# A channel mixer in two token halves, with gate and up products in Strassen's form, on one Trainium2 core

## Chip, cores and metric

One core of a Trainium2 chip runs the whole program. Its engines run side by side: TensorE (PE: matmuls; PEld: its weight loads), VectorE (DVE), ScalarE (ACT), GpSimd (POOL), and SyncE (SP), which here issues the DMAs. The metric is the time of one execution on the device in microseconds (us); lower is better. TensorE's granted clock has two levels, 1.2 and 2.4 GHz; the profile gives it as a share of the upper one.

## What is computed

Two layers over 1152 tokens (128 prompt and 1024 sample tokens) of 1024 features. Each layer is a token mixer (latent attention, short convolution, retention, not changed in what it computes) and a SwiGLU channel mixer with 2816 hidden features, both with a modulated norm and a gated residual:

```
def _swiglu(h, w_gate, w_up, w_down):
    return (jax.nn.silu(h @ w_gate) * (h @ w_up)) @ w_down
...
xs = xs + g1 * mix
xs = xs + g2 * _swiglu(_modulate(_rmsnorm(xs, norm2_g[l]), sh2, sc2), *ffn)
```

Everything is float32; prompt tokens have another modulation (shift, scale, gate) than sample tokens.

## The kernel before

Activations lie feature-major: a tile is 128 features by 1152 tokens, and the residual x is 8 such tiles. Each large product runs as three matmuls on operands that were split into a rounded part and a rest, hi and lo (type float32r): `mm3` (L189 to L194) issues hi*hi, hi*lo and lo*hi for each 128 features of the contraction and adds them up in a PSUM tile. A matmul's moving operand is a chunk of 384 tokens; there are three chunks, taken in the order 1, 2, 0 at a phase's boundaries.

Weights come in tiles of 128 x 1024 from a queue written out by hand (`order`, L93). `prep_next` (L142) loads the next one on SP, copies it to hi on ACT (L169) and subtracts on POOL to get lo (L170); `get` keeps one more key prepared than the one in use. The tiles rotate through a pool of 7 (`W`); activations rotate through a pool of 34 slots of 128 x 1152 (`S`), small pieces through 8 temporaries (`Tt`). PSUM's eight banks are two pools, `mm` (3) and `ax` (5).

The channel mixer has 22 hidden tiles in groups of 2 or 3. `gate_up` (L1291) makes one hidden tile: three gate products of 24 matmuls each, with silu on ACT (L1280), then three up products, multiplied in on DVE (L1285), and split on ACT (L1286) and DVE (L1287). After a group has been made, `down` (L1306) adds the group before it to the residual: for each of 8 output tiles and 3 chunks one PSUM tile of 6 or 9 matmuls, and one or two DVE operations (`resid`, L1200; two for chunk 0, where prompt and sample tokens have different gates). The order in which the engines get their instructions is that of a scheduler which follows the program's order but lets a later instruction go first where, by its own estimate, an earlier one still waits.

`boundary` (L1237) carries the three chunks through the end of one phase (`rows_tail`, the last products that are added to the residual), the norm (squares on ACT, sums on DVE and POOL L391, 1/sqrt in small DVE steps L201 to L206, spread over the partitions by PE L247), its application (L422 to L429), and the first products of the next phase. It is used twice in a layer: from the output projection to the channel mixer, and from the channel mixer to the next layer. In layer 0's mixer the modulations of layer 1 are computed on the side (`tick`, `ada_work`).

Of the kernel before, what the change touches and what calls it, by code (L numbers as in the profile page):

```python
# [29 lines left out]
GROUPS = [2, 3, 3, 3, 3, 3, 3, 2]  # L30
EPS = 1e-6
SCALE = 96.0 ** -0.5
NS, NW = 34, 7          # slots of [128, 1152] and of [128, 1024]
# [10 lines left out]
M0, M1, M2 = 3, 5, 6  # L44


def segs(c):
    if c == 0:
        return [(0, 128, 0), (128, 384, 1)]
    return [(c * CH, (c + 1) * CH, 1)]  # L50


class Net:
    def __init__(self, ctx, tc, a, o):
# [5 lines left out]
        self.tp = pool("temps", bufs=8)  # L60
# [32 lines left out]
    def order(self):  # L93
        q = []
        for l in range(L):
            q += [("in", l, i) for i in range(len(IN_FM))]
            q += [("woa", l, m) for m in range(8)] + [("wob", l, j) for j in range(2)]
            h = 0
            for gi, g in enumerate(GROUPS):
                for i in range(g):  # L100
                    if h != 1:
                        q += [("gate", l, h), ("up", l, h)]
# [16 lines left out]
    def wsrc(self, key):  # L119
# [8 lines left out]
        if k == "gate":  # L128
            return a["w_gate"][l, key[2]], 1024
# [1413 lines left out]
```

## Time and profile before

| | us |
|---|---|
| median of three runs | 3245.52 |
| lowest, highest run | 3243.17, 3247.36 |
| the profiled execution, first to last instruction (span) | 3242.0 |
| TensorE busy in the span | 3136.6 (97%) |
| VectorE busy | 1407.3 (43%) |
| ScalarE busy | 956.3 (29%) |
| GpSimd busy | 860.1 (27%) |

The page gives the profiled execution by its span; the timed runs lie 1.2 to 5.4 us above it. A busy share is that of one engine over the whole span. A matmul's row shows a start and a modelled duration; matmuls overlap in the pipeline, so the step from one start to the next is what a matmul costs. The same holds, in a smaller measure, for DVE.

### The profile page before, as it was taken

What the parts mean: (1) busy time and instruction counts of PE and PEld (TensorE: products, weight loads), DVE (VectorE), ACT (ScalarE), POOL (GpSimd) and SP (SyncE); (2) the same over time, 40 slices, a digit from 0 to 9 for tenths busy, and PEclk for the clock granted to TensorE, in tenths of its full rate; (3) what the DMA queues carried; (4) which work ended last, traced back from release to release, by engine and by line L of the source; (5) the groups of instructions that cost most, each with busy time, mean ns of one, the idle gap of its engine ahead of it and who ended that gap; (6) DMA issues with size and microseconds to landing.
All of it is one profiled execution on the core that took longest, in us unless ns stands there. A gap on an engine that the chain in (4) does not pass through costs nothing.

```text
span 3242.0 us, 43302 instructions
## 1 busy us (share of the span) xinstructions
PE 3136.6 (97%) x17680; PEld 2785.3 (86%) x17680; DVE 1407.3 (43%) x2914; ACT 956.3 (29%) x2388; POOL 860.1 (27%) x469
## 2 busy tenths in 40 slices
PE   6999989999999999999999999899999999999999
PEld 5988755578999999999989896555889999999999
DVE  6254576745422212312373646767364222223323
ACT  4433455433311111111144234454342111111110
POOL 3101344553212111211141113435441112111211
PEclk8999999999999999999999999999999999999999
DMA  5223100121121222222131110001211111111112
GB/s 212 99 72 127 34 12 16 36 101 45 46 77 61 71 82 69 65 80 76 60 119 34 33 53 12 12 30 59 76 34 33 35 49 41 40 43 49 40 40 85
DMA packets 75302, 191.18 MB, mean 59 GB/s; under 512 B 7264, under 2 KB 33632, under 8 KB 75104
## 3 DMA queue, kind: packets, MB, share of 16 engines
q1 hardware_dynamic: 75104, 188.42, 17.5%
q8 instruction: 139, 2.28, 0.3%
q14 instruction: 59, 0.48, 0.0%
HBM read 171.45 MB, written 16.94 MB: 58 GB/s over the span
## 4 chain that ended last, share of the span: by engine, by line
PE 87%; DVE 9%; ACT 2%; issue 1%; DMA 1%; SPq 0%; POOL 0%; ACTq 0%; POOLq 0%; DVEq 0%
PE mm L192 22%; PE mm L194 22%; PE mm L193 22%; PE ax L1071 5%; PE ax L1042 2%; PE mm L1088 2%; PE mm L1090 2%; PE mm L1089 2%; PE ax L303 1%; PE ax L1031 1%; DVE mx L1044 1%; PE ax L247 1%; DMA aw<-in_ada_w 1%; PE ax L921 1%; DVE rst L205 1%
## 5 line engine op out<-in xcount | busy, mean ns | idle before, releaser
L192 PE MATMUL mm<-hh,W 128*128 128x384 f32 x2720 | 919.8, 338 | 0.0
L194 PE MATMUL mm<-hh,W 128*128 128x384 f32 x2720 | 914.9, 336 | 0.0
L193 PE MATMUL mm<-hl,W 128*128 128x384 f32 x2720 | 914.6, 336 | 0.2
L170 POOL TENSOR_TENSOR W<-W,W 128x1024 fp32r<-128x1024 f32 (+1 forms) x190 | 420.5, 2213 | 1687.8 <-ACT W L169 1523.8
L192 PEld LDWEIGHTS mm<-hh,W 128*128 128x128 f32 x2720 | 513.1, 189 | 24.0 <-issue 17.3
L193 PEld LDWEIGHTS mm<-hl,W 128*128 128x128 f32 x2720 | 513.4, 189 | 2.2 <-POOL hl L429 0.8
L194 PEld LDWEIGHTS mm<-hh,W 128*128 128x128 f32 x2720 | 513.3, 189 | 1.3 <-issue 1.0
L1200 DVE SCALAR_TENSOR_TENSOR x<-mm,mod,x 128x384 f32<-128x384 f32 (+2 forms) x640 | 314.9, 514 | 367.5 <-PE mm L194 367.2
L169 ACT CAST W<-W 128x1024 fp32r<-128x1024 f32 (+1 forms) x190 | 185.8, 978 | 874.8 <-PE mm L193 797.8
L1285 DVE TENSOR_TENSOR sil<-sil,mm 128x384 f32<-128x384 f32 x132 | 73.0, 553 | 822.3 <-PE mm L194 820.5
L192 PE MATMUL mm<-gh,W 128*128 128x384 f32 x1056 | 353.9, 335 | 3.9 <-DVE x L1200 3.9
L194 PE MATMUL mm<-gh,W 128*128 128x384 f32 x1056 | 352.9, 334 | 1.2 <-POOL W L170 1.2
L193 PE MATMUL mm<-gl,W 128*128 128x384 f32 x1056 | 352.9, 334 | 0.0
L1080 POOL TENSOR_TENSOR pacc<-pacc,W 128x1024 f32<-128x1024 f32 x96 | 230.6, 2402 | 216.1 <-ACT W L1091 205.2
L1044 DVE TENSOR_REDUCE mx<-ax 128x1 f32<-128x384 f32 x384 | 195.0, 549 | 107.8 <-PE ax L1042 105.7
L1091 ACT ACTIVATE W<-mm 128x512 f32<-128x512 f32 x288 | 169.5, 607 | 211.8 <-PE mm L1090 198.8
L1071 PE MATMUL ax<-W,vt 128*64 128x512 f32 x576 | 204.6, 649 | 8.2 <-DVE attn L1123 6.7
L192 PEld LDWEIGHTS mm<-gh,W 128*128 128x128 f32 x1056 | 198.2, 188 | 8.7 <-issue 3.3
L194 PEld LDWEIGHTS mm<-gh,W 128*128 128x128 f32 x1056 | 198.2, 188 | 1.5 <-POOL W L170 1.5
L193 PEld LDWEIGHTS mm<-gl,W 128*128 128x128 f32 x1056 | 198.3, 188 | 0.0
L1286 ACT CAST gh<-sil 128x384 fp32r<-128x384 f32 x132 | 67.5, 511 | 343.3 <-DVE sil L1285 343.3
L1287 DVE TENSOR_TENSOR gl<-sil,gh 128x384 fp32r<-128x384 f32 x132 | 134.3, 1017 | 76.9 <-ACT gh L1286 76.9
(276 smaller groups left out, 4173.5 us busy)
## 6 DMA issues: line engine op xcount, KB each, us to landing
W<-in_ada_w SPq DMA_DIRECT2D x80, 512.0 KB, 4.0
W<-in_w_gate SPq DMA_DIRECT2D x44, 512.0 KB, 3.6
W<-in_w_up SPq DMA_DIRECT2D x44, 512.0 KB, 3.6
W<-in_w_down SPq DMA_DIRECT2D x48, 384.0 KB, 3.3
W<-in_w_in_fm SPq DMA_DIRECT2D x30, 512.0 KB, 3.9
aw<-in_ada_w SPq DMA_DIRECT2D x16, 512.0 KB, 8.4
mr<-spill SPq DMA_DIRECT2D x12, 576.0 KB, 4.8
W<-in_w_oa SPq DMA_DIRECT2D x16, 384.0 KB, 3.1
```

What stands on the lines that cost most here:

```text
L169: self.nc.scalar.copy(hi, raw)
L170: self.nc.gpsimd.tensor_tensor(lo, raw, hi.bitcast(F32), op=ALU.subtract)
L192: self.nc.tensor.matmul(ps, wh, xh, start=first and i == 0, stop=False)
L193: self.nc.tensor.matmul(ps, wh, xl, start=False, stop=False)
L194: self.nc.tensor.matmul(ps, wl, xh, start=False, stop=last and i == n - 1)
L1044: nc.vector.reduce_max(mx[:, qt, c:c + 1], ps, axis=AX.X)
L1071: nc.tensor.matmul(po[64 * qc:64 * qc + 64, :], vv[:, kt, b:b + 64], prs[kt][:, qs], start=(kt == 0), stop=(kt == 8))
L1080: nc.gpsimd.tensor_tensor(acc, acc, prs[kt], op=ALU.add)
L1091: nc.scalar.activation(pr[:, qs], ps, AF.Exp, scale=SCALE)
L1200: self.nc.vector.scalar_tensor_tensor(x[m][:, t0:t1], ps[:, t0 - c * CH:t1 - c * CH], self.mod[l][:, j, m, i:i + 1], x[m][:, t0:t1], ALU.m ...
L1285: nc.vector.tensor_tensor(sil, sil, ps, op=ALU.mult)
L1287: nc.vector.tensor_tensor(lo[:, s], sil, hi[:, s].bitcast(F32), op=ALU.subtract)
```

## The change

1. The channel mixer goes over 576 tokens at a time (half 1, tokens 576 to 1151, then half 0), and over all 22 hidden tiles, in 11 pairs, for each half. All its weights are loaded and split once for each half. Each half is two blocks of 288 tokens; in half 0 each block takes 64 prompt and 224 sample tokens.
2. Gate and up: a pair of hidden tiles (2 x 128), the contraction in two halves of 512 features, and the two blocks of 288 tokens make a 2 x 2 by 2 x 2 block product. `gate_up` computes it in Strassen's form (Winograd's variant): seven block products of 4 x 3 matmuls of 288 columns, and the additions behind them on DVE. The sums of weight blocks (S1 to S4) are made on DVE for each unit (`prep_unit`), those of activation blocks (T1 to T4) once for each half (`half_apply`).
3. Down and the last part of the output projection run in 288 columns, a pair of hidden tiles at a time (`rows_tail`): PSUM tiles of 6 matmuls.
4. The boundary to the mixer is `mixer`: the norm for half 1 is applied while the projection's last part runs for half 0; that for half 0 during the last two pairs' down products of half 1.
5. Pools: 32 slots instead of 34, 12 weight tiles instead of 7, 9 temporaries instead of 8. Retention's tables, the token-major input weights (three pieces instead of two), and attention's query tiles and sums move from slots to weight tiles. The weight tiles that were prepared in slots for the mixer's start (`prep_slots`) are gone.

```diff
-NS, NW = 34, 7          # slots of [128, 1152] and of [128, 1024]
+HW = 288
+HORDER = (1, 0)
+NP = HID // 2
+NS, NW = 32, 12
...
+COLS = [[[(0, 64, 0, 0), (128, 352, 64, 1)], [(64, 128, 0, 0), (352, 576, 64, 1)]],
+        [[(576, 864, 0, 1)], [(864, 1152, 0, 1)]]]
+NSP = [[(0, 352), (352, 224)], [(576, 288), (864, 288)]]
...
+            for H in HORDER:
+                for p in range(NP):
+                    q += [("unit", l, H, "gate", p)]
+                    if 0 < p < NP - 1:
+                        q += [("dn", l, H, p - 1)]
+                    q += [("unit", l, H, "up", p)]
+                q += [("dn", l, H, NP - 2), ("dn", l, H, NP - 1)]
...
+    def prep_unit(self, l, name, p):
+        V = self.nc.vector
+        r1, r2 = (self.S("raw", (P, 1024)) for _ in range(2))
+        for j, r in enumerate((r1, r2)):
+            self.load(r, self.a["w_" + name][l, 2 * p + j])
+        a, b = slice(0, 512), slice(512, 1024)
+        s1, s2, s3, s4 = (self.Tt("ws", (P, 512)) for _ in range(4))
+        V.tensor_tensor(s1, r2[:, a], r2[:, b], op=ALU.add)
+        V.tensor_tensor(s2, s1, r1[:, a], op=ALU.subtract)
+        V.tensor_tensor(s3, r1[:, a], r2[:, a], op=ALU.subtract)
+        V.tensor_tensor(s4, r1[:, b], s2, op=ALU.subtract)
+        W = {}
+        hi, lo = self.hilo(r1, self.W(F32R), self.W(F32R))
+        W["A11"], W["A12"] = (hi[:, a], lo[:, a]), (hi[:, b], lo[:, b])
+        for n1, n2, x1, x2 in (("S1", "S2", s1, s2), ("S3", "S4", s3, s4)):
+            hi, lo = self.W(F32R), self.W(F32R)
+            W[n2] = self.hilo(x2, hi[:, b], lo[:, b])
+            W[n1] = self.hilo(x1, hi[:, a], lo[:, a])
+        w = self.W(F32R)
+        W["A22"] = self.hilo(r2[:, b], w[:, a], w[:, b])
+        return W
...
+    def rows_tail(self, l, j, x, H, groups, paired, out=None):
+        for gi, (ws, act) in enumerate(groups):
             for m in range(KD):
+                d = slice(m * P, (m + 1) * P)
+                for c in range(2):
+                    ps = self.mm((P, HW))
...
+                    self.mm3(ps, terms)
+                    self.resid_half(x, m, ps, l, j, H, c, paired)
...
+    def half_apply(self, l, x, H, ys, h):
+        R = [self.rms_rows(y, 1, w) for y, (_, w) in zip(ys, NSP[H])]
+        ab, mod = self.ab[l][:, 1], self.mod[l][:, 3]
+        for kp in range(4):
+            b = self.S("hb", (P, 4, HW))
+            for e in range(2):
+                k = kp + 4 * e
+                for c in range(2):
+                    for t0, t1, p0, i in COLS[H][c]:
+                        n = 0 if t1 <= NSP[H][1][0] else 1
+                        o = t0 - NSP[H][n][0]
+                        nc.vector.scalar_tensor_tensor(b[:, (1 - c, 2 + c)[e], p0:p0 + t1 - t0], x[k][:, t0:t1],
+                                                       ab[:, k, i:i + 1], R[n][:, o:o + t1 - t0], ALU.mult, ALU.mult)
...
+            t = self.S("ht", (P, 4, HW))
+            B12, B11, B21, B22 = (b[:, i] for i in range(4))
+            V.tensor_tensor(t[:, 0], B12, B11, op=ALU.subtract)
+            V.tensor_tensor(t[:, 1], B22, t[:, 0], op=ALU.subtract)
+            V.tensor_tensor(t[:, 2], B22, B12, op=ALU.subtract)
+            V.tensor_tensor(t[:, 3], B21, t[:, 1], op=ALU.subtract)
+            th, tl = self.hilo(t, self.S("hth", (P, 4, HW), F32R), self.S("htl", (P, 4, HW), F32R))
...
+            for i0, i1, hi, lo in cuts:
+                nc.scalar.copy(hi, b[:, i0:i1])
+                V.tensor_tensor(lo, b[:, i0:i1], hi.bitcast(F32), op=ALU.subtract)
...
+    def gate_up(self, W, h, first=False):
+        out = self.S("gu", (P, 4, HW))
+        c11, c12, c21, c22 = (out[:, i] for i in range(4))
+        m1, u2, t5, t7 = (self.Tt("u", (P, HW)) for _ in range(4))
+        add = lambda o, x, ps: V.tensor_tensor(o, x, ps, op=ALU.add)
+        def p1(ps):
+            nc.scalar.copy(m1, ps)
+        def p7(ps):
+            add(t7, u2, ps)
+            add(c22, t5, ps)
+        todo = [("A11", "B11", p1), ("A12", "B21", lambda ps: add(c11, m1, ps)), ("S2", "T2", lambda ps: add(u2, m1, ps)),
+                ("S1", "T1", lambda ps: add(t5, u2, ps)), ("S3", "T3", p7), ("S4", "B22", lambda ps: add(c12, t5, ps)),
+                ("A22", "T4", lambda ps: add(c21, t7, ps))]
+        n = 4 if first else 1
+        for i0 in [0] + list(range(n, 7)):
+            some = todo[i0:i0 + (n if i0 == 0 else 1)]
+            ps = [(self.mm if (i0 + i) % 2 else self.ax)((P, HW)) for i in range(len(some))]
+            for k in range(4):
+                d = slice(k * P, (k + 1) * P)
+                for p, (a, b, _) in zip(ps, some):
+                    self.mm3(p, [(W[a][0][:, d], W[a][1][:, d], *h[k][b])], k == 0, k == 3)
...
+    def mixer_half(self, l, x, H, h, out=None):
...
+        for p in range(NP):
+            g = self.gate_up(self.get(("unit", l, H, "gate", p)), h, p == 0)
+            self.nc.scalar.activation(g, g, AF.Silu)
+            if 0 < p < NP - 1:
+                for _ in self.rows_tail(l, 5, x, H, [group(p - 1)], True):
+                    pass
+            u = self.gate_up(self.get(("unit", l, H, "up", p)), h)
+            self.nc.vector.tensor_tensor(g, g, u, op=ALU.mult)
+            gs[p] = hi, lo = [self.S("gs", (P, 4, HW), F32R) for _ in range(2)]
+            self.nc.scalar.copy(hi, g)
+            self.nc.vector.tensor_tensor(lo, g, hi.bitcast(F32), op=ALU.subtract)
...
+    def mixer(self, l, x, o_tail):
+        a, b = HORDER
+        for _ in zip(o_tail(a), self.half_sq(x, a, sa)):
+            pass
+        qb = self.half_sq(x, b, sb)
+        for m, _ in enumerate(o_tail(b)):
+            if m == 1:
+                ya = self.half_rsq(a, sa)
+            if m == 2:
+                ga = self.half_apply(l, x, a, ya, ha)
+            if m > 2:
+                next(ga, None)
+            next(qb)
...
+        yb = self.half_rsq(b, sb)
+        tail = self.mixer_half(l, x, a, ha, out)
+        gb = self.half_apply(l, x, b, yb, hb)
...
+        for i, _ in enumerate(tail):
+            if i % 4 == 0:
+                next(gb)
...
+        tail = self.mixer_half(l, x, b, hb, out)
+        if l + 1 < L:
+            self.R = self.in_start(l + 1)
```

## Rows read from the trace of the kernel before

**Rows 1.** The page, parts 1 and 4: busy time by engine, the chain by engine

```profile
PE 3136.6 (97%) x17680; PEld 2785.3 (86%) x17680; DVE 1407.3 (43%) x2914; ACT 956.3 (29%) x2388; POOL 860.1 (27%) x469
...
PE 87%; DVE 9%; ACT 2%; issue 1%; DMA 1%; SPq 0%; POOL 0%; ACTq 0%; POOLq 0%; DVEq 0%
```

**Rows 2.** Busy time by stretch (us, busy and count per engine, clock, DMA), layer 1

```profile
2296.00:2372.00 76.00, 76.00 (x436) 74.47 (x433) 26.87 (x42) 12.81 (x18) 21.55 (x11) 1.00 0.19 60
2372.00:2404.00 32.00, 28.48 (x167) 27.32 (x166) 26.62 (x57) 14.97 (x27) 13.54 (x13) 1.00 0.05 17
...
2413.00:2418.30 5.30, 5.25 (x18) 5.25 (x19) 3.48 (x7) 2.79 (x6) 0.58 (x1) 0.50 0.24 87
2420.00:3242.00 822.00, 817.22 (x4718) 816.61 (x4716) 243.61 (x431) 140.88 (x234) 156.79 (x76) 1.00 0.14 45
```

**Rows 3.** TensorE in order of time (start, us): first and last of 46 matmuls, 384 columns

```profile
1701.57 0.34 PE L194 MATMUL mm<-hh,W 128*128 128x384 f32 x1
...
1709.38 0.33 PE L194 MATMUL mm<-hh,W 128*128 128x384 f32 x1
```

**Rows 4.** The same, right behind: first and last of 23 matmuls, 288 columns

```profile
1709.55 0.29 PE L785 MATMUL mm<-twh,hh 128*128 128x288 f32 x1
...
1712.47 0.29 PE L786 MATMUL mm<-twl,hh 128*128 128x288 f32 x1
```

**Rows 5.** TensorE in order of time, layer 1, output projection to the end

```profile
2296.47 0.45 PE L192 MATMUL mm<-mh,W 128*128 128x384 f32 x1
...
2404.16 0.41 PE L192 MATMUL mm<-hh,W 128*128 128x384 f32 x1
...
2413.05 1.65 PE L247 MATMUL ax<-ident,rsy 128*128 128x128 f32 x6 [3.46 <-DVE rsy L206]
...
2414.82 0.52 PE L192 MATMUL mm<-hh,W 128*128 128x384 f32 x1
...
2418.32 0.34 PE L194 MATMUL mm<-hh,W 128*128 128x384 f32 x1
...
3238.14 0.34 PE L194 MATMUL mm<-gh,W 128*128 128x384 f32 x1
```

**Rows 6.** VectorE's groups by line and shape: count, busy us, mean ns, idle before

```profile
L1200 DVE SCALAR_TENSOR_TENSOR x<-mm,mod,x 128x384 f32<-128x384 f32 x320 | 196.7, 617 | 243.8 <-PE mm L194 243.5
...
L1200 DVE SCALAR_TENSOR_TENSOR x<-mm,mod,x 128x256 f32<-128x256 f32 x160 | 75.8, 474 | 0.0
L1285 DVE TENSOR_TENSOR sil<-sil,mm 128x384 f32<-128x384 f32 x132 | 73.0, 553 | 822.3 <-PE mm L194 820.5 <-ACT sil L1280 1.8
L1200 DVE SCALAR_TENSOR_TENSOR x<-mm,mod,x 128x128 f32<-128x128 f32 x160 | 55.7, 348 | 123.7 <-PE mm L194 123.7
```

**Rows 7.** VectorE in order of time, layer 1, mixer's start

```profile
2405.32 2.38 DVE L427 SCALAR_TENSOR_TENSOR hl<-xn,mod,hh 128x384 fp32r<-128x384 f32 x1 [0.53 <-ACT hh L423]
...
2411.86 0.16 DVE L204 TENSOR_TENSOR rst<-rsy 128x3 f32<-128x3 f32 x1
...
2412.84 0.16 DVE L206 SCALAR_TENSOR_TENSOR rsy<-rst,rsy 128x3 f32<-128x3 f32 x1
2414.82 1.66 DVE L422 SCALAR_TENSOR_TENSOR xn<-x,ab,ax 128x384 f32<-128x384 f32 x3 [1.82 <-PE ax L247]
2416.40 0.61 DVE L427 SCALAR_TENSOR_TENSOR hl<-xn,mod,hh 128x384 fp32r<-128x384 f32 x1
```

**Rows 8.** GpSimd in order of time, same place

```profile
2404.89 2.40 POOL L170 TENSOR_TENSOR W<-W,W 128x1024 fp32r<-128x1024 f32 x1
```

**Rows 9.** GpSimd's groups by line and shape

```profile
L170 POOL TENSOR_TENSOR W<-W,W 128x1024 fp32r<-128x1024 f32 x126 | 301.2, 2390 | 1167.3 <-ACT W L169 1008.8 <-PE ax L303 63.1 <-PE mm L194 58.7
...
L1078 POOL TENSOR_TENSOR pacc<-pacc,W 128x512 f32<-128x512 f32 x16 | 21.1, 1316 | 13.8 <-ACT W L1091 13.0
```

**Rows 10.** The page: GB/s in 40 slices (part 2), a weight tile's load (part 6)

```profile
GB/s 212 99 72 127 34 12 16 36 101 45 46 77 61 71 82 69 65 80 76 60 119 34 33 53 12 12 30 59 76 34 33 35 49 41 40 43 49 40 40 85
...
W<-in_w_gate SPq DMA_DIRECT2D x44, 512.0 KB, 3.6
```

More of the change, by code (lines that the diff above doesn't have):

```diff
@@ L50, in segs, with span, subs @@
     return [(c * CH, (c + 1) * CH, 1)]
+def span(c):
+    return (c * CH, CH) if isinstance(c, int) else c
+def subs(w):
+    return [min(o, w - P) for o in range(0, w, P)]
+COLS = [[[(0, 64, 0, 0), (128, 352, 64, 1)], [(64, 128, 0, 0), (352, 576, 64, 1)]],
+        [[(576, 864, 0, 1)], [(864, 1152, 0, 1)]]]
+NSP = [[(0, 352), (352, 224)], [(576, 288), (864, 288)]]
 class Net:
@@ L59, in __init__ @@
         self.wp = pool("weights", bufs=2)
-        self.tp = pool("temps", bufs=8)
+        self.tp = pool("temps", bufs=9)
         self.mp = pool("small", bufs=2)
@@ L226, in rms_sum @@
         pc = pc.rearrange("p a b -> p (a b)")
-        for j in range(3):
-            self.nc.tensor.matmul(pc, sq[:, j * P:(j + 1) * P], self.unit[:, t0 + j, :pc.shape[1]],
-                                  start=first and j == 0, stop=last and j == 2)
+        ss = subs(sq.shape[1])
+        for j, o in enumerate(ss):
+            self.nc.tensor.matmul(pc, sq[:, o:o + P], self.unit[:, t0 + j, :pc.shape[1]],
+                                  start=first and j == 0, stop=last and j == len(ss) - 1)
     def rms_bcast(self, pc, inv):
@@ L238, in rms_rsq, with rms_rows @@
         return self.rsq(ms, (P, n))
-    def rms_rows(self, y, heads=1):
+    def rms_rows(self, y, heads=1, width=CH):
         nc = self.nc
-        R = self.ax()[:, :CH]
+        R = self.ax()[:, :width]
+        if heads == 1:
+            for j, o in enumerate(subs(width)):
+                nc.tensor.matmul(R[:, o:o + P], y[:, j:j + 1].to_broadcast([P, P]), self.ident,
+                                 start=True, stop=True)
+            return R
         w = P // heads
@@ L382, in norm_sq_steps @@
         nc = self.nc
-        s = slice(c * CH, (c + 1) * CH)
+        t0, w = span(c)
+        s = slice(t0, t0 + w)
         sqs = []
         for k in range(KD):
-            t = self.Tt("sq")
+            t = self.Tt("sq", (P, w))
             nc.scalar.activation(t, x[k][:, s], AF.Square)
@@ L500, in retention @@
         dm, qdec, kdec, cdec = self.ret_tables(l)
-        ss = [self.S("sst", (P, 8, 2, 64)) for _ in range(2)]
+        ss = [self.Wv((P, 8, 2, 64)) for _ in range(2)]
         st = self.a["state_ret"]
@@ L1220, in w_o @@
             last.append((hi, lo))
-        return self.rows_tail(l, 2, x, [self.get(("wob", l, j), ahead=0) for j in range(2)], last)
-    def rows_tail(self, l, j, x, ws, acts, out=None):
-        def tail(c):
-            s = slice(c * CH, (c + 1) * CH)
+        ws = [self.get(("wob", l, j), ahead=0) for j in range(2)]
+        return lambda H: self.rows_tail(l, 2, x, H, [(ws, lambda jj, c, H: tuple(
+            t[:, H * 2 * HW + c * HW:H * 2 * HW + (c + 1) * HW] for t in last[jj]))], False)
@@ new lines, in mixer_half, with group, tail @@
+    def mixer_half(self, l, x, H, h, out=None):
+        gs = {}
+        def group(p, ahead=1):
+            ws = self.get(("dn", l, H, p), ahead)
+            gh, gl = gs.pop(p)
+            return ws, lambda jj, c, H: (gh[:, 2 * jj + c], gl[:, 2 * jj + c])
+        for p in range(NP):
[9 more added lines that the diff above has]
+            self.nc.vector.tensor_tensor(lo, g, hi.bitcast(F32), op=ALU.subtract)
+        def tail():
+            for p in (NP - 2, NP - 1):
+                yield from self.rows_tail(l, 5, x, H, [group(p)], True, out if p == NP - 1 else None)
+        return tail()
```

315 lines of the change are left out of this document (141 added, 174 removed).

## The prediction

> **What bounds the kernel now.** I read the page's busy times and the chain that ended last first: TensorE is busy 97% of the span and is 87% of the chain, VectorE 9%; VectorE, ScalarE and GpSimd are busy 43, 29 and 27% [rows 1]. An average can hide stages, so next the stretches of layer 1: in the channel mixer TensorE is busy 817.2 of 822.0 us, and only around the mixer's start does it fall behind, 28.5 of 32.0 us [rows 2]. So the mixer, which is two times some 820 us, costs what its matmuls cost one behind the other; a change in it is worth the change in count times step, less what its new edges lose. The step is read from starts, not durations: 45 steps of 384 columns take 7.81 us, 0.1735 us each [rows 3]; 22 steps of 288 columns take 2.92 us, 0.1327 us [rows 4]. Of the durations (0.33 and 0.29 us) three quarters of the columns would seem to save little; of the steps they save 23.5%. The 288-column rows are the token-major input products, float32r with new weights before each matmul like the mixer's, so I take them for the new form, rounded up to 0.1331.
>
> Layer 1's stretch from the output projection's first matmul to the last matmul's end is 2296.47 to 3238.48, 942.0 us [rows 5]. Its products are 432 of the projection, 144 of its last part and 4752 of the mixer, 5328 x 0.1735 = 924.4. The other 17.6 us are the start: the norm's small products and waits, the longest 3.46 us on the 1/sqrt steps, behind which the clock is granted at 0.50 (the lower level, 1.2 GHz) and a step is twice as long, from 2413 to 2418.3 [rows 2, 5].
>
> **The change part by part, both layers.**
>
> Gate and up: before 22 tiles x 2 x 3 chunks x 24 matmuls x 2 layers = 6336, at 0.1735 = 1099.3 us. After, 11 pairs x 2 x 7 products x 12 matmuls x 2 halves x 2 layers = 7392 of 288, at 0.1331 = 983.9. Seven for eight would be 12.5%; it is 10.5%, since a step shrinks less than its columns: **-115.4**.
>
> Down: 3168 x 0.1735 = 549.6 becomes 4224 x 0.1331 = 562.2: **+12.6**. The projection's last part: 288 x 0.1735 = 50.0 becomes 384 x 0.1331 = 51.1: **+1.1**. TensorE's products in sum: **-101.7**. This needs no cover, TensorE being the bound; what follows is what takes it back.
>
> VectorE's prices: operations in a row start closer than they last: three of 0.61 us (L422, L427) take 1.66 us together, 0.525 each, so I take 0.085 off each duration [rows 7]. A residual step (617, 474 and 348 ns for 384, 256 and 128 columns [rows 6]) is then 0.43 us for 288, 0.36 for 224, 0.19 for 64. A two-input sum (553 ns for 384 [rows 6]) is 0.37 for 288, 0.60 for 512, 0.97 for 864, 1.26 for 1152.
>
> Steady state: a pair of hidden tiles has 264 matmuls, 35.1 us. VectorE in it: eight weight sums 4.8, fourteen additions behind products 5.2, product and rest 2.5, sixteen residual steps 6.9 in half 1 and 16 x 0.55 = 8.9 in half 0: 19.4 to 21.4 us. GpSimd: for each unit one 1024-wide rest and five 512-wide, at 2.39 and 1.32 [rows 9] 9.0 us, and two down rows 4.8: 22.7 us. Neither is the bound. A down phase alone (96 matmuls, 12.8 us, PSUM tiles of 0.80 us, three of them) leaves VectorE 0.37 and 0.25 us a tile beside the residual steps, and 2.4 us of weight sums can fall into it: 9.3 to 11.3 of 12.8. Bounds: nothing, or the four sums in one block, 2.4 us against the 1.6 us that two spare PSUM tiles cover, 1.2 us in each of 36 phases, 43 us. Since VectorE has 14 us free in each pair and the scheduler puts sums where it waits, I take 0.2 us each: **+8** (0 to 43).
>
> Mixer's start. On VectorE, while TensorE runs the two half-parts of the projection (192 matmuls, 25.6 us): residual steps 6.9 + 8.9, square sums 16 x 0.37 = 5.9, two 1/sqrt chains of 12 steps, 0.196 us apart [rows 7], 4.7, weight sums 2.4, and for each of four steps of half_apply four products 1.7, four differences 1.5 and a rest 0.97, 16.7 in all: 45.5 us. As a chain: squares to 14, 1/sqrt to 19, spread to 20.5, then half_apply with the rest of half 0's work between, to 48.5, and the last piece's copy and GpSimd rest, 52. The first products are interleaved over the contraction so that three quarters of four (4.8 us) can go ahead: 52 - 30.4 = 22 us lost, and some 2 for the clock behind it, 24 against 17.6 now, so **+7** a layer, +14 (bounds -8 to +40: the old start's loss halved, and each step held by GpSimd once).
>
> Between the halves there was no edge before. VectorE: 2.5 + 32 residual steps 13.8 + weight sums 2.4 + half_apply for half 0 (eight short products 2.2, differences 1.5, rest 0.97, times four: 18.6): 37 us, against 25.6 of down products and again 4.8. That is 7 us, and 4 for the last piece's copy and rest, less the first piece, which free slots let run under the last up product: 6, and 2 of clock: **+8** a layer, +16 (0 to 40).
>
> Layer 0's end: VectorE has 37 us in the last 25.6 us of products (residual steps 17.8, the second chunk's norm 8, squares, sums), and the twelve weight tiles are short there: six hold the next input weights and four a down pair, so the second rest of the last pair waits for the pair before it. The old boundary there lost some us too. **+6** (-3 to +15). Layer 0's modulations take two weight tiles of 12 at a time, where a unit (7), a down pair (up to 6) and they make more than 12: **+4** (0 to 20).
>
> Loads: a pair needs six times 512 KB in 35.1 us, 90 GB/s, where the first slice moved 212 GB/s and one load lands in 3.6 us [rows 10]: hidden; without that cover a unit would be late by one load, 3.6 us. ScalarE's copies (3584 columns a unit) are a third of the time: hidden. Attention, retention and the input projection keep their work; their moved tiles I put at 0, within 8 either way, since I see no row that prices a pool's size.
>
> Sum: -101.7 + 8 + 14 + 16 + 6 + 4 = -53.7. The span was 3242.0; 3188.3, and the median lies 3.5 above the span: 3191.8, say **3191**.
>
> **The shared reads of VectorE and GpSimd.** A VectorE step with two SBUF inputs (L427) takes 0.61 us, and 2.38 when it starts under a GpSimd rest of 2.40 us: it ended 0.4 us after that rest [rows 7, 8]. The new mixer has ten such steps in each pair of hidden tiles and GpSimd busy 22.7 of 35.1 us. The Trainium skill says it as a rule (SBUF — State Buffer, "Who interferes with whom"): such a step and a GpSimd instruction that reads SBUF exclude each other for a whole instruction. Its other half, that GpSimd is held by VectorE too, no row here shows; by it GpSimd would have 22.7 + 8.3 of 35.1 us. The residual steps and the additions behind products have one input in PSUM and keep one duration, so only the ten are at stake. This is the first rival.
>
> **Rivals.**
> 1. Slower: held steps in the down phases. If the weight sums fall into the down phases and each is held by a rest (1.5 us on average over 2.39 and 1.32), a block of four lasts 8 us, of which PSUM covers 1.6; the following residual steps can't win TensorE's time back. Half of that, 3 us in each of 44 pairs, is 132 us, against the 8 in my sum: 3191 + 124 = 3315. It decides from (54 + 8)/44 = 1.4 us a pair on. For it: 2.38 against 0.61. Against: sums are due a whole unit ahead, and the rests of a unit come behind its sums.
> 2. Weights late: the pool of 12 and the 32 slots can't hold two units, a down pair and the side work. 1.1 us for each of 44 pairs: 3191 + 48 = 3239. For it: 7 + 6 is over 12. Against: a unit's tiles come free product by product.
> 3. The edges cost no more than now: the sum without the 14, 16, 6 and 4, down to half the 8: 3152. For it: VectorE was busy 26.6 of 32.0 us there already [rows 2] and TensorE lost little. Against: both edges have more VectorE work than TensorE work.
>
> **How the numbers follow.** Forecast 0.62 (3165 to 3225 from the edge terms), rival 1 0.16, rival 2 0.12, rival 3 0.10. The range goes from rival 3 to the near half of rival 1: 3150 to 3275. With 0.2% (6.5 us, about what can be told from no change) faster takes the forecast, rival 3 and half of rival 2, 0.78; the same 0.05 and slower 0.17 are the rest of rivals 2 and 1.
>
> **What would show it.** Steps of 0.133 us in long runs of 288 columns at clock 1.00 (the first term; at 0.15 the gain is gone); an unbroken pair of 35.1 us; mixer stretches of some 774 us of products in layer 1; VectorE near full and TensorE waiting on it for some 20 us at the mixer's start and some 8 between the halves; weight sums (512 columns) near 0.7 us, not 2. I am wrong if TensorE waits inside the pairs (for residual steps: rival 1; for weight rests: rival 2), or if attention's stretches move by more than 8 us.

## The result, and the profile after

The changed kernel takes 3442.68 us (median of four runs, 3434.03 to 3447.16) beside 3244.81 for the kernel before on the same chip: a ratio of 1.0608 [1.0589 to 1.0627], slower, where 3191 was forecast and the range ended at 3275. The profiled span is 3432.3 us, 190.3 longer.

The page, part 1 (busy us, share of the span, instructions), of the changed kernel. TensorE is busy for as long as before [rows 1], but for 91% of the span; VectorE and GpSimd are busy for 850 and 762 us more:

```profile
PE 3137.3 (91%) x19904; PEld 2750.0 (80%) x19904; DVE 2257.0 (66%) x4404; ACT 1259.8 (37%) x2778; POOL 1622.5 (47%) x932
```

Between TensorE's first matmuls of each stage, the time by stretches (the last column is the fastest kernel of the experiments below):

| us of the span | before | after | best (e14) |
|---|---|---|---|
| start to layer 0's projection | 687.4 | 705.3 | 708.6 |
| layer 0's projection and mixer, layer 1's inputs | 1279.2 | 1362.2 | 1280.7 |
| layer 1's attention | 329.8 | 337.6 | 336.9 |
| layer 1's projection and mixer, to the end | 945.5 | 1027.1 | 922.9 |

So 164 us of the loss lie in the two mixers, 26 in stages that the change was not meant to touch.

**The products.** TensorE in order of time, layer 1, the first and last of 168 matmuls, an up unit and the next gate unit of 84 each (start, us):

```profile
2603.44 0.29 PE L216 MATMUL ax<-hx,W 128*128 128x288 f32 x1
...
2625.62 0.29 PE L218 MATMUL ax<-hth,W 128*128 128x288 f32 x1
```

That is 167 steps in 22.18 us, 0.1328 each, as [rows 4] had it. There is no gap. The products do save 102 us. That TensorE's busy time is no shorter than before is due to longer steps elsewhere: in the table's last stretch, steps beyond 0.1735 and 0.1328 us add 46 us (4 before), besides 98 us of idle time (8 before).

**The down phase behind it** should take 12.8 us and takes 15.9, from 2625.75 to 2641.63. TensorE's last matmul ahead of the gap and the first behind it (in brackets: idle us, and what ended it):

```profile
2628.01 0.29 PE L218 MATMUL mm<-gs,W 128*128 128x288 f32 x1
2630.83 0.40 PE L216 MATMUL mm<-gs,W 128*128 128x288 f32 x1 [2.53 <-DVE x L1264]
```

VectorE in the same stretch. The weight sums (L175 to L178) are all of 512 columns and two SBUF inputs:

```profile
2623.56 2.43 DVE L175 TENSOR_TENSOR ws<-raw 128x512 f32<-128x512 f32 x1
2625.91 0.44 DVE L1383 TENSOR_TENSOR gu<-u,mm 128x288 f32<-128x288 f32 x1
2626.28 0.68 DVE L176 TENSOR_TENSOR ws<-ws,raw 128x512 f32<-128x512 f32 x1
2626.88 1.78 DVE L177 TENSOR_TENSOR ws<-raw,raw 128x512 f32<-128x512 f32 x1
2628.59 0.44 DVE L1383 TENSOR_TENSOR gu<-u,ax 128x288 f32<-128x288 f32 x1
2628.95 1.39 DVE L178 TENSOR_TENSOR ws<-raw,ws 128x512 f32<-128x512 f32 x1
2630.26 0.93 DVE L1264 SCALAR_TENSOR_TENSOR x<-mm,mod,x 128x288 f32<-128x288 f32 x2
```

ScalarE copies each sum as soon as it is made, and GpSimd takes the rest behind the copy:

```profile
2626.08 0.62 ACT L201 CAST W<-ws 128x512 fp32r<-128x512 f32 x1 [4.76 <-DVE ws L175]
2626.99 0.62 ACT L201 CAST W<-ws 128x512 fp32r<-128x512 f32 x1 [0.29 <-DVE ws L176]
```

```profile
2623.04 2.41 POOL L202 TENSOR_TENSOR W<-raw,W 128x1024 fp32r<-128x1024 f32 x1
2626.78 6.42 POOL L202 TENSOR_TENSOR W<-ws,W 128x512 fp32r<-128x512 f32 x4 [1.34 <-ACT W L201]
```

A sum that starts in the gap between two rests takes 0.68 us (2626.28). One that starts under a rest is held: it ends about 0.5 us behind that rest, 2625.99 after 2625.45. It is the behaviour of [rows 7, 8]. Over the run, 132 of the 352 sums start with no GpSimd instruction under way and take 0.67 to 0.69 us; the other 220 start under one and take 1.71 us in the mean. The additions with one input in PSUM (0.44 us) are not touched, but they and the residual steps stand behind the held sum: the first residual step comes 4.5 us after the down phase began, and three PSUM tiles are 2.4 us of work. VectorE's groups over the whole run (count, busy us, mean ns, idle before):

```profile
L175 DVE TENSOR_TENSOR ws<-raw 128x512 f32<-128x512 f32 x88 | 141.8, 1612 | 7.0 <-DMA raw<-in_w_up 4.2 <-DMA raw<-in_w_gate 2.8
L177 DVE TENSOR_TENSOR ws<-raw,raw 128x512 f32<-128x512 f32 x88 | 138.3, 1572 | 0.0
...
L178 DVE TENSOR_TENSOR ws<-raw,ws 128x512 f32<-128x512 f32 x88 | 106.9, 1214 | 0.0
...
L176 DVE TENSOR_TENSOR ws<-ws,raw 128x512 f32<-128x512 f32 x88 | 79.3, 901 | 1.2
```

TensorE's waits, whole run (us in total, times, longest): the first line is this wait.

```profile
PE mm L216 <- DVE x L1264: 113.2, 61, 4.3
PE ax L253 <- DVE sq L424: 37.5, 6, 14.9
PE ax L216 <- ACT W L201: 36.3, 3, 17.3
```

There are 36 down phases beside running pairs. In 26 of them the 96 matmuls stand in a row; these take 17.04 us in the mean, not 12.8: 4.2 each. Where the granted clock is 1.00 over the phase, it takes 15.9 to 16.1 us; at 0.90 16.9 to 17.3, at 0.81 or 0.82 18.4 to 19.0. The mixers make four passes over a half of the tokens, nine such phases each. By TensorE's steps, the three passes without modulations lose 116 us, of which 75 are waits and 41 longer steps. In half 1 of layer 0 the modulations' products stand between, and the waits for residual steps are only 8 us (ten times).

**The edges**, by stretches of layer 1 (length, busy us and count by engine, clock, DMA): the last part of the projection, and the first part of the down products between the halves.

```profile
2496.24:2539.00 42.76, 16.78 (x116) 15.58 (x114) 39.39 (x123) 18.48 (x33) 13.57 (x10) 0.75 0.21 74
2948.88:2991.50 42.62, 31.13 (x193) 29.25 (x192) 34.79 (x75) 17.72 (x27) 22.42 (x11) 0.88 0.13 50
```

VectorE is busy for 92 and 82% of them while TensorE waits. At the start two waits follow each other, for half 0's square sums and for the first unit's copy on ScalarE, which stood behind half_apply's last piece:

```profile
2522.05 2.29 PE L253 MATMUL ax<-unit,sq 128*128 128x3 f32 x10 [8.25 <-DVE sq L424]
2541.67 0.61 PE L216 MATMUL ax<-hx,W 128*128 128x288 f32 x1 [17.32 <-ACT W L201]
```

Behind the second the granted clock is 0.50, the lower level (1.2 GHz), for 5 us, in which eight matmuls run (the stretch's row, columns as above):

```profile
2541.67:2547.00 5.33, 2.42 (x8) 1.85 (x8) 5.30 (x4) 0.70 (x2) 4.05 (x3) 0.50 0.00 0
```

From the projection's first matmul to the end of the first 252 gate and up products the products are 134.0 us; the stretch (2405.16 to 2584.43) takes 179.3, a loss of 45. Between the halves 84.1 us are taken for 59.1 of products, a loss of 25 (32 in layer 0).

### The profile page after: what moved, and what is told of

It is laid out like the page before. It is cut to its first block, busy times and chain, and to the rows that moved or that the text cites. A ratio compares the mean times of both kernels' runs of the same rounds, so it can differ in the third digit from the quotient of the medians.

```text
span 3432.3 us, 51706 instructions
## 1 busy us (share of the span) xinstructions
PE 3137.3 (91%) x19904; PEld 2750.0 (80%) x19904; DVE 2257.0 (66%) x4404; ACT 1259.8 (37%) x2778; POOL 1622.5 (47%) x932
## 5 line engine op out<-in xcount | busy, mean ns | idle before, releaser
L202 POOL TENSOR_TENSOR W<-W,W 128x1024 fp32r<-128x1024 f32 (+3 forms) x144 | 345.3, 2402 | 632.9 <-ACT W L201 309.5
L202 POOL TENSOR_TENSOR W<-ws,W 128x512 fp32r<-128x512 f32 x352 | 512.3, 1486 | 78.6 <-ACT W L201 71.9
L216 PE MATMUL mm<-gs,W 128*128 128x288 f32 x1408 | 445.4, 316 | 107.3 <-DVE x L1264 106.0
L1264 DVE SCALAR_TENSOR_TENSOR x<-mm,mod,x 128x64 f32<-128x64 f32 (+2 forms) x1136 | 425.6, 413 | 106.2 <-PE mm L218 95.9
L202 POOL TENSOR_TENSOR W<-raw,W 128x1024 fp32r<-128x1024 f32 (+1 forms) x176 | 341.4, 1942 | 314.9 <-issue 244.0
L218 PE MATMUL mm<-gs,W 128*128 128x288 f32 x1408 | 434.9, 309 | 2.3 <-POOL W L202 2.3
L217 PE MATMUL mm<-gs,W 128*128 128x288 f32 x1408 | 435.6, 309 | 0.0
L216 PEld LDWEIGHTS mm<-gs,W 128*128 128x128 f32 x1408 | 284.4, 202 | 125.8 <-DVE x L1264 60.6
L218 PE MATMUL ax<-hth,W 128*128 128x288 f32 x1056 | 314.2, 298 | 6.7 <-POOL W L202 6.7
L216 PE MATMUL ax<-hth,W 128*128 128x288 f32 x1056 | 315.0, 298 | 2.7 <-ACT W L201 1.6
L217 PE MATMUL ax<-htl,W 128*128 128x288 f32 x1056 | 313.7, 297 | 0.0
L217 PEld LDWEIGHTS mm<-gs,W 128*128 128x128 f32 x1408 | 284.7, 202 | 2.5 <-issue 2.5
L218 PEld LDWEIGHTS mm<-gs,W 128*128 128x128 f32 x1408 | 283.5, 201 | 3.7 <-POOL W L202 2.9
L216 PE MATMUL mm<-hh,W 128*128 128x384 f32 x704 | 240.8, 342 | 0.0
L218 PE MATMUL mm<-hh,W 128*128 128x384 f32 x704 | 240.0, 341 | 0.0
L217 PE MATMUL mm<-hl,W 128*128 128x384 f32 x704 | 239.2, 340 | 0.0
```

Of the source, the lines that this page charges most:

```text
L202: self.nc.gpsimd.tensor_tensor(lo, raw, hi.bitcast(F32), op=ALU.subtract)
L216: self.nc.tensor.matmul(ps, wh, xh, start=first and i == 0, stop=False)
L217: self.nc.tensor.matmul(ps, wh, xl, start=False, stop=False)
L218: self.nc.tensor.matmul(ps, wl, xh, start=False, stop=last and i == n - 1)
L1264: self.nc.vector.scalar_tensor_tensor(x[m][:, t0:t1], ps[:, p0:p0 + t1 - t0], self.mod[l][:, j, m, i:i + 1], x[m][:, t0:t1], ALU.mult, ALU ...
```

## Experiments

Each kernel is the changed one with the edit shown, except e7; from e9 on edits are added up. "Ratio" is to the kernel before, with its 95% interval. The theory is that the down phases' loss is held weight sums. The rivals are too much work on VectorE, too few PSUM tiles, and late weights.

**e1: more PSUM tiles** in the down phases and the projection's last part.

```diff
-                    ps = self.mm((P, HW))
+                    self.flip = 1 - getattr(self, "flip", 0)
+                    ps = (self.mm if self.flip else self.ax)((P, HW))
```

> Down products take their PSUM tiles in turn from both pools (eight tiles instead of three); all else as changed. Theory A (VectorE comes some 4 us late into each down phase, behind weight sums, and three PSUM tiles of 0.8 us can't cover that): the waits of down products for the residual steps (113 us in the changed kernel) nearly go, a down phase of 96 matmuls falls from 16 to 18.6 us to about 13, and with 36 of them and the edges the time falls by 120 to 160 us, to 3290 to 3320. Theory B (VectorE has more work in a down phase than the phase is long, so any number of tiles fills up): a phase stays above 15 us and the time falls by less than 50 us.

3321.31, ratio 1.0235 [1.0205 to 1.0264]: 121 us come back. Down phases take 13.7 us, though the sums are still long (L175 1758 ns). So PSUM cover hides the holds; whether they are holds it doesn't say.

**e2: no weight sums** (S1 to S4 aren't computed; raw blocks are split in their place).

```diff
+        s1, s2, s3, s4 = r2[:, a], r1[:, a], r2[:, a], r1[:, b]
```

> The weight sums S1 to S4 are left out: blocks of the loaded tiles are split in their place (the products are of other matrices, as many as before). Copies, rests, loads and products stay. Theories A and B alike: down phases of 12.8 to 13.2 us, 3280 to 3310. If something other than the sums holds the residual steps (the rests or copies, the loads), phases stay above 15 us and the time above 3400.

3303.31, ratio 1.0180 [1.0142 to 1.0218]. Down phases take 12.75 us with three PSUM tiles: the sums are the cause, by their number or by their length.

**e3: sums kept, no hold.** GpSimd's rests of gate and up weights become two memsets (the lo parts are left out).

```diff
+        self.blank = True
...
+        if getattr(self, "blank", False):
+            for _ in range(2):
+                self.nc.gpsimd.memset(lo.bitcast(F32), 0.0)
+        else:
+            self.nc.gpsimd.tensor_tensor(lo, raw, hi.bitcast(F32), op=ALU.subtract)
```

> The rests of gate and up weights on GpSimd are replaced by two memsets of the same tile, which read nothing (so these weights have no lo part; the sums on VectorE stay). Theory A with the shared reads as its root: the sums take 0.6 to 0.7 us each instead of up to 2.9, a down phase 12.8 to 13.5 us, time 3290 to 3330. Theory B, or if the number of sums and not their being held matters: sums shorter, but phases still above 15 us, 3400 or more.

3290.56, ratio 1.0140 [1.0102 to 1.0179]. All 352 sums are there at 683 to 685 ns, and the down phases of the three passes without modulations take 12.75 us, nearly all with their 96 matmuls in a row: it is the sums' length. TensorE's waits for residual steps (line numbers are six higher here) fall from 113.2 us:

```profile
PE mm L222 <- DVE x L1270: 31.3, 25, 4.3
```

```profile
L175 DVE TENSOR_TENSOR ws<-raw 128x512 f32<-128x512 f32 x88 | 60.2, 684 | 4.4 <-DMA raw<-in_w_up 4.4
L178 DVE TENSOR_TENSOR ws<-raw,ws 128x512 f32<-128x512 f32 x88 | 60.1, 683 | 0.0
```

**e4: the first unit's weights ahead of half_apply.**

```diff
             if m == 2:
+                while not self.ready:
+                    self.prep_next()
                 ga = self.half_apply(l, x, a, ya, ha)
```

> The first unit's weights are asked for before the norm of the first half is applied, instead of behind it. Theory: at the mixer's start TensorE stands 17.3 us for the first unit's ScalarE copy, which is queued behind the norm's last pieces though its data landed 20 us earlier; asked for earlier, the first products run beside the norm and the start gets 8 to 14 us shorter in each layer: 3415 to 3428. Rival: the norm's last piece is due at the same time anyway and the sums of that unit only delay it: no change within 5 us.

3426.36, ratio 1.0559 [1.0511 to 1.0607], 16 us below the changed kernel, but of two runs that lie 16 us apart, and the intervals overlap. In layer 1 the 17.3 us wait for the copy is gone, but the stretch of 179.3 us is still 174.2: what the first products gain is mostly lost again on residual steps (15.3 us in six waits). Layer 0's start is 4 us shorter.

**e5: e1, the first unit's weights still earlier** (`prep_next` right after the projection's last weights) **and half 0's norm inside the first unit.**

```diff
+        self.prep_next()
         return lambda H: ...
...
             self.tick()
+            next(self.late, None)
```

> Eight PSUM tiles for the down products (as in e1_psum8), the first unit's weights asked for in the output projection, and the squares and 1/sqrt of the second half moved from the mixer's start into its first unit. If the start is long because VectorE has some 45 us of work there and the first weights queue behind it, taking 6 to 10 us of work away and the weights' wait (12.7 us in e1_psum8) shortens each start by 12 to 20 us: 3280 to 3300 against 3321 of e1_psum8. Rival: what counts at the start is the chain norm, 1/sqrt, four pieces, one after the other, and the moved work only filled gaps: 3310 to 3321.

3309.07, ratio 1.0204 [1.0178 to 1.0229], 12 us below e1: 1 us below the rival's range, 9 above the theory's. With the squares moved away the loss turns up among the first products.

**e6: e1 with the rests of gate and up weights on VectorE** instead of GpSimd.

```diff
-        self.nc.gpsimd.tensor_tensor(lo, raw, hi.bitcast(F32), op=ALU.subtract)
+        (eng or self.nc.gpsimd).tensor_tensor(lo, raw, hi.bitcast(F32), op=ALU.subtract)
```

> As e1_psum8, with the rests of gate and up weights (one 1024-wide, five 512-wide a unit) on VectorE instead of GpSimd; nothing is left out. If being held is what makes the sums long, VectorE can carry the rests itself (about 8 us a pair more, 30 of 35 us) and no longer waits for GpSimd: down phases of 12.8 to 13.5 us and a time at or below that of e1_psum8, 3290 to 3321. If VectorE's amount of work is the limit, phases grow to 15 us and more and the time to 3360 or above.

3304.06, ratio 1.0184 [1.0155 to 1.0214]. VectorE has more work (2370 us busy against 2238 in e1) and the run is not slower.

**e8: the same edit with three PSUM tiles**, so without e1.

> The changed kernel with one edit: the rests of the gate and up weights (per unit one of 1024 columns and five of 512) on VectorE instead of GpSimd. Three PSUM tiles in the down phases, as in the changed kernel; nothing is left out. VectorE gets about 4 us more in each unit. Theory (VectorE's two-input steps are held by GpSimd's rests): the sums are short again, down phases of 13 to 14.5 us instead of 17.0, the run 3305 to 3345. Rival (VectorE has too much work for three PSUM tiles, whichever engine holds it): down phases stay at 16 us or more and the run above 3400.

3310.54, ratio 1.0203 [1.0170 to 1.0236]: 132 us back with nothing left out and three tiles, the time as the theory had it. The sums are short:

```profile
L202 DVE TENSOR_TENSOR W<-raw,W 128x1024 fp32r<-128x1024 f32 x88 | 108.4, 1231 | 5.7 <-ACT W L201 5.6
...
L175 DVE TENSOR_TENSOR ws<-raw 128x512 f32<-128x512 f32 x88 | 60.4, 686 | 2.9 <-DMA raw<-in_w_up 2.0 <-DMA raw<-in_w_gate 0.9
...
L177 DVE TENSOR_TENSOR ws<-raw,raw 128x512 f32<-128x512 f32 x88 | 60.1, 683 | 0.0
```

The row of one pair in layer 1 (busy by engine, clock) shows TensorE without a gap and VectorE at 88% of the time:

```profile
2577.00:2612.00 35.00, 35.00 (x266) 35.00 (x266) 30.72 (x53) 12.33 (x19) 4.98 (x2) 1.00 0.25 91
```

Most pairs take 35.03 us, where the prediction had 35.1; in the changed kernel 38.2 to 41.3. The amount of VectorE's work was not the limit, nor were late weights. But the order is another: here the scheduler puts 24 to 36 products of the up unit into a down phase, most of them behind its first three PSUM tiles, so that a phase lasts 15.9 to 17.5 us from its first matmul to its last, 12.75 of them its own. That three tiles are enough for a phase in one piece is shown by e2 and e3, not by e8.

**e7: the pools alone.** The kernel *before*, with the change's part 5 (32 slots, 12 weight tiles, 9 temporaries, the moved tables and query tiles) and `dynamic_dma_scratch_size=1024`, which the changed kernel has too and the list of the change doesn't name.

> The kernel before with the pools' part of the change alone (32 slots, 12 weight tiles, 9 temporaries; retention's tables, attention's query tiles and sums and the token-major weights in weight tiles); its channel mixer stays. The changed kernel needs 17.9 us more up to the first output projection and 11.2 us more from the second layer's start to its own. If the pools do that, the same stretches are 14 to 20 and 8 to 14 us longer here than before, 3265 to 3285 in all (more if the mixer lacks slots). If they come from elsewhere (order of loads, code), the stretches are as before within 3 us.

3260.61, ratio 1.0046 [1.0027 to 1.0065]: some 15 us, less than expected. The trace is of the slowest of its four runs (3271.79; the others 3258.53 to 3262.21). In it the loss lies ahead of the mixers: 713.0 us to layer 0's projection (687.4 before, 705.3 changed) and 338.7 in layer 1's attention (329.8 and 337.6), while the other two stretches of the table are 3 to 4 us shorter each.

**e9: e5 and e6 together.**

> The changed kernel with the edits that gained so far together: PSUM tiles of the down phases from both pools, the weight rests on VectorE, the first unit's weights prepared before half_apply, and half 0's norm moved into the first unit. Nothing is left out. Theory (the losses are separate places): the two gains behind the PSUM tiles, 12 and 17 us, add up: 3321 less 29 is 3292, within 10. Rival (the start is bound by VectorE's amount of work, and the rests now stand there too): no more than the rests alone, 3300 to 3310. Either way not below the kernel before, since pools and the two edges of each layer stay.

3293.76, ratio 1.0157 [1.0130 to 1.0184]: close to the sum of both.

**e10: e9, with a third pair's down products held back** to the end of half 1.

```diff
-            if 0 < p < NP - 1:
+            if 0 < p < (NP - 2 if H else NP - 1):
```

> The combined kernel with one more edit: in half 1 the down products of the ninth pair wait until the last unit has been made, so that 288 instead of 192 matmuls (38.3 instead of 25.6 us) lie beside VectorE's work between the halves. Theory (VectorE's 37 us against TensorE's 25.6 make the loss between the halves): 12.8 us more cover less 6.9 us of residual steps that come along, 6 us a layer, so 10 to 14 us below the combined kernel. Rival (the loss is the chain behind the last product, its copy and rest, or the slots that the late pair holds): no gain, or some us more.

3290.84, ratio 1.0141 [1.0119 to 1.0163]: no gain outside the intervals, the rival's case.

**e11: e9, with half 0's sums T1 to T4 on GpSimd.**

```diff
-            V.tensor_tensor(t[:, 0], B12, B11, op=ALU.subtract)
+            (nc.gpsimd if H == 0 else V).tensor_tensor(t[:, 0], B12, B11, op=ALU.subtract)
```

> The combined kernel with one more edit: half 0's sums T1 to T4 of activation blocks on GpSimd instead of VectorE, 1.5 us of VectorE's for each of four pieces, 6 us a layer. Theory (steps of the two engines hold each other): VectorE's own two-input steps between the halves, products and rests, get longer by more than the 6 us, so the run is 0 to 20 us above the combined kernel. Rival (only the amount of VectorE's work counts there): 8 to 12 us below it.

3298.19, ratio 1.0165 [1.0132 to 1.0198]: 4 us above e9, the intervals overlap. Not the rival's gain of 8; more isn't settled.

**e12: e10, with half_apply's pieces every sixth step** (`i % 6` for `i % 4`).

> The kernel with the ninth pair held back between the halves, with one more edit: the four pieces of half_apply for half 0 are begun every sixth step of the 24 instead of every fourth, so that they lie along the whole 38 us. Nothing is left out. Theory (the added cover brought nothing because all four pieces still stood in the first 16 steps, where residual steps wait behind them): some 8 to 15 us below that kernel's 3291, the loss between the halves from some 23 us a layer to 15 or less. Rival (the loss is the chain behind the last piece): within 3 us of it, or slower since the last piece now ends later.

3285.87, ratio 1.0131 [1.0106 to 1.0156]: 5 us below e10, the intervals overlap. Between the halves 18.6 us are still lost in layer 1 (20.3 in e10).

**e13: e12 (without the early weights), the projection's chunk 0 behind half 1's last part**, so that 25 us more of TensorE's work lie beside half_apply.

```diff
+        for _ in part("woa", (2, 1)):
+            pass
...
+        return part("woc", (0,)), lambda H: ...
```

> The same kernel with one more edit, at the mixer's start: the output projection makes the chunks 2 and 1 for all eight rows first, then the last part for half 1, and only then chunk 0 (its eight weight tiles are loaded and split a second time), so that 144 matmuls, 25 us of TensorE, lie beside half 1's norm and half_apply, besides the 12.8 us of half 0's last part. The mixed inputs are split by chunks for that. Nothing is left out. Theory (the start's loss of 31 to 35 us a layer is TensorE without work while VectorE makes half 1's operands): the first 252 products of a mixer take 33.5 to 43 us instead of 64 to 69, and the run falls by 40 to 55 us, to 3225 to 3250, the kernel before's 3245 or just below. Rival (the chain of copies, sums and rests and the clock behind it would stay): 10 to 20 us at most.

3267.75, ratio 1.0072 [1.0047 to 1.0097]: 18 us, less than half of what was expected and in the rival's range. The stretch of 179.3 us (175.4 in e12) is now 163.7. In this trace half_apply's own rests are long, each beside a GpSimd rest of `htl` (2665 ns):

```profile
L1381 DVE TENSOR_TENSOR hz<-hb,hz 128x576 fp32r<-128x576 f32 x8 | 21.9, 2742 | 0.5
...
L1381 DVE TENSOR_TENSOR hy<-hb,hx 128x864 fp32r<-128x864 f32 x8 | 20.2, 2528 | 2.9 <-ACT hx L1380 2.8
```

**e14: e13, with those `htl` rests on VectorE too.**

```diff
-            th, tl = self.hilo(t, self.S("hth", ...), self.S("htl", ...))
+            th, tl = self.hilo(t, self.S("hth", ...), self.S("htl", ...), nc.vector)
```

> The kernel with chunk 0 of the projection held back, with one more edit: in half_apply the rests of the sums T1 to T4 (1152 columns) on VectorE instead of GpSimd. Nothing is left out. In its trace VectorE's own rests in half_apply took 2.74 us for 576 columns and 2.53 for 864, each beside such a GpSimd rest of 2.66; unheld they should take 0.8 and 1.1. Theory (held steps are part of the edges' loss too): those two fall to 0.8 and 1.1 us, VectorE gains 7 us a half and pays 4 x 1.4 = 5.6, the last piece's chain is 1.3 us shorter: 5 to 12 us below the 3268 over four edges. Rival (only VectorE's amount counts): within 3 us.

3251.39, ratio 1.0022 [1.0008 to 1.0036]: 16 us, more than expected, by giving VectorE more instructions. The 576 columns take 754 ns. The added rests (21.7 us) cost VectorE about what the holds had (23.5), so the gain is not in its amount of work. Of the 16 us, 11 lie in the four edges (the two stretches at the starts and those between the halves); 4 lie ahead of layer 0's projection, which the edit doesn't touch:

```profile
L202 DVE TENSOR_TENSOR htl<-ht,hth 128x1152 fp32r<-128x1152 f32 x16 | 21.7, 1358 | 1.1 <-ACT hth L201 1.1
...
L1381 DVE TENSOR_TENSOR hy<-hb,hx 128x864 fp32r<-128x864 f32 x8 | 12.6, 1578 | 0.0
...
L1381 DVE TENSOR_TENSOR hz<-hb,hz 128x576 fp32r<-128x576 f32 x8 | 6.0, 754 | 0.0
```

**e15: e14, half 0's last part ahead of chunk 0, and the first unit's weights between.**

```diff
+        self.first = self.get(("unit", l, a, "gate", 0), ahead=0)
+        for m, _ in enumerate(o_rest):
+            if m % 2 == 0:
+                next(ga, None)
```

> The same as that kernel with the order at the start changed once more: the last part of the projection for half 0 comes ahead of chunk 0's products, and the first unit's weights are prepared between the two, so that half_apply's last pieces have the 25 us of chunk 0 beside them and the 7 us of weight sums and rests aren't in their way. Nothing is left out. Theory (order on VectorE's queue, not its amount, makes what is left of the start's loss, some 25 us a layer): 15 to 30 us below the kernel with the rests moved, 3230 to 3250, level with the kernel before or just below. Rival (VectorE is full there in any order): within 5 us.

3273.90, ratio 1.0090 [1.0070 to 1.0110], worse than e14 by more than either theory had it. In layer 1 the first unit's products, which now come ahead of chunk 0's, wait 9.3 us for copies on ScalarE (once 8.0), and chunk 0's products four times for their weights' rests on GpSimd (4.1 us).

**e16: e14, half_apply begun two rows earlier. e17: e16, the first unit's weights asked for later.**

```diff
-            if m == 3:
+            if m == 2:
                 ga = self.half_apply(l, x, a, ya, ha)
-            if m > 3:
+            if m > 1:
                 next(ga, None)
```

> The kernel with the T rests on VectorE, with one more edit: half_apply for half 1 begins two rows of the projection's chunk 0 earlier (at the third row, not the fifth), 6 us. Nothing is left out. In its trace VectorE stood idle for some 5 us ahead of the first piece, and TensorE waited once for 7.4 us on residual steps behind half_apply and the first unit's sums. Theory (what is left of the start is order on VectorE's queue): 3 to 4 us a layer, 4 to 10 us below the 3251, so level with the kernel before or just below it. Rival (the first piece can't start earlier, 1/sqrt being its chain): within 3 us.

> The same with one more edit: the first unit's weights are asked for in the middle of half 0's last part of the projection, not ahead of it, so that their 8 us of sums and rests on VectorE don't stand ahead of its residual steps. Nothing is left out. Theory (the 7.4 us wait is that block of sums): the wait goes, the first products wait for the weights for some 3 to 5 us instead: 0 to 10 us below the other kernel of this pair. Rival (the sums are on the chain of the first products, so that later is worse): 5 to 15 us above it.

3255.56 and 3252.00, ratios 1.0025 [1.0016 to 1.0034] and 1.0027 [1.0015 to 1.0038]: both level with e14. The 7.4 us wait is gone in e16 already. The start's stretch takes 162 us there in layer 1 and 158 in layer 0, 160 in both layers in e14.

No version beats the kernel before. The best, e14, has layer 1's mixer stretch 22.7 us below that kernel's; it loses 28 us in the stages ahead of the mixers and 1.5 in layer 0's stretch (table above).

## Why the prediction was wrong

**Products, -101.7:** right, step by step (0.1328).

**Steady state, +8 (0 to 43): the step that failed.** It measured some +120: 116 us in the 27 phases of three passes, and 4 to 7 in half 1 of layer 0, by which that half gets shorter in e8 and e3. "Since VectorE has 14 us free in each pair and the scheduler puts sums where it waits, I take 0.2 us each" priced the sums at 0.60 us and asked only if VectorE had room. It had: in e8 there is room for the rests as well. What counts is how long the steps last that stand together ahead of a residual step. A sum that starts under a rest takes 1.4 to 2.4 us in the rows above, and two or three such steps in a row outlast three PSUM tiles. In the sum of means the four sums of a unit cost 5.30 us instead of 2.74 in e8. The bound of 43 us had a slip besides: 2.4 us less 1.6 is 0.8, not 1.2. The phases also lose more than the waits, since in most of them the granted clock is below 1.00; the prediction counted that for the edges only.

**Rival 1 (0.16) was the mechanism.** The Trainium skill has its rule for VectorE steps with two SBUF inputs beside GpSimd steps that read SBUF (SBUF — State Buffer, "Who interferes with whom"). This trace agrees, 2.43 us against 0.68 for one shape. The rival's price was near: 3 us a pair guessed, 4.2 measured in a phase; that its time of 3315 is still 128 us short is due to the other terms below. It got its low chance from "sums are due a whole unit ahead, and the rests of a unit come behind its sums". In the trace they are mixed: the first rest of a unit (2623.04) needs no sum and runs beside its first one, and the rest of each sum runs beside the sums behind it. e2, e3 and e8 each take away another part of the pair (the sums, the rests' reading, the rests' engine), and in each the down phases of these three passes take 12.75 us of their own, but for a few. For GpSimd held in turn the prediction set 8.3 us a pair; ten steps at its own prices are 7.3, or 8.2 with the 0.085 us that it took off. It used the figure nowhere.

**Mixer's start, 24 us a layer:** 45. VectorE's 45.5 us of work were about right (39.4 us busy in 42.8, holds included), but two things came on top: half_apply's held rests, 1.8 and 1.9 us in the mean and up to 2.9 (only the far bound, +40, had "each step held by GpSimd once"), and the first unit's copy, which ScalarE's order put behind half_apply. e4 took the copy's wait away (4 and 5 us of the two starts), e14 the holds (2 and 4); e13 gave the rest something to hide behind (18 us in all).

**Between the halves, 8 us a layer:** 25. Part of it are the same held rests (e14: 2.7 us a layer). The 37 us of VectorE's work beside 25.6 of TensorE's were not all: 12.8 us more of TensorE's work changed nothing that can be measured (e10). What sets the 19 and 16 us that e14 still loses there in layers 0 and 1 is open.

**Layer 0's end and modulations, +10:** too little for the modulations, which cost some 20 us more than before. The stretches of the two layers lost about the same, 83.0 and 81.6 us, but half 1 of layer 0 lost only 8 us to waits for residual steps. Without holds it takes 378.7 us (e3) and 381.9 (e8), and layer 1's half 1 326.8 and 326.7: the modulations cost 52 to 55 us there. In the kernel before, where they lie along the whole mixer, that mixer takes some 34 us more than its products. Why they cost more now wasn't tried; the end of layer 0 was not measured by itself.

**Unchanged stages, 0 within 8:** +26. The pools cost 15 us by themselves (e7), with shorter mixers set against it; in the trace of e7 the same two stages lose 34. Which of the sizes does it wasn't tried.

For layer 1: -50.8 (products) + 79.6 (18 down phases) + 27.6 (start, 45.2 less the old 17.6) + 25.1 (between) + 1.4 (last tail) is +82.9, against 81.6 in the table.

## What to carry over

Before work goes to an engine that has room, ask what else its steps can wait for: price a VectorE step with two SBUF inputs by the longest GpSimd instruction that may stand beside it, and compare that with what its followers have in PSUM cover. A rest of 512 columns took 684 ns on VectorE and 1486 on GpSimd (1297 where no such VectorE step stood beside it), so GpSimd was no cheap place for it; adding PSUM tiles hid the same loss without removing it. And a pool that is re-cut for one stage can be paid for in others: run that part by itself.

## What was not expected of the hardware

GpSimd's own rests got longer. The 512-wide ones had 1316 ns [rows 9]; beside VectorE's sums four of them in a row need 6.42 us (above), and over the run:

```profile
L202 POOL TENSOR_TENSOR W<-ws,W 128x512 fp32r<-128x512 f32 x352 | 512.3, 1486 | 78.6 <-ACT W L201 71.9 <-PE ax L218 6.6
```

Of these 352 rests, 171 run beside none of VectorE's weight sums, products and rests and take 1.30 us in the mean; the other 181 take 1.67. So the hold goes both ways, which the prediction had left open. And it isn't only for steps with two SBUF inputs: a copy of three columns (one input) that starts under a GpSimd rest took 2.62 us and ended with it, where one of two columns with no GpSimd step beside it took 0.17:

```profile
2530.84 2.62 DVE L1331 COPY yh<-rsy 128x3 f32<-128x3 f32 x1
...
2533.76 0.17 DVE L1331 COPY yh<-rsy 128x2 f32<-128x2 f32 x1
```

```profile
2530.82 2.62 POOL L202 TENSOR_TENSOR htl<-ht,hth 128x1152 fp32r<-128x1152 f32 x1 [5.68 <-ACT hth L201]
```
